# The ring of weights of a two-layer encoder: raw tiles of 1024 columns in three buffers instead of 2048 in two, and three split buffers instead of two

## The chip, the cores and the metric

The kernel runs on one core of a Trainium2 chip. The metric is the device time of one execution in microseconds (us), lower is better; the median of three runs is given. The engines are named as in the profile: PE is TensorE (matmuls), PEld its loads of the stationary operand, DVE VectorE, ACT ScalarE, POOL GpSimd, SP the queue that issues the DMAs.

## The reference

Two layers act on 512 tokens of width 1024, all in float32. Each layer is a gated feed-forward block, a mixer, and a second feed-forward block:

```python
for l in range(DEPTH):                                   # DEPTH = 2
    x = x + 0.5 * swiglu(rmsnorm(x, ffn1_norm[l]), ffn1_w_gate[l], ffn1_w_up[l], ffn1_w_down[l])
    h = rmsnorm(x, mix_norm[l])
    u = h @ w_in[l]
    ...
    y_conv = short_conv_mixer(c_x, c_b, c_c, conv_w[l])
    y_rwkv = rwkv7_mixer(rw_r, rw_k, rw_v, ...)          # a recurrence over the tokens, both directions
    y_ret = retention_mixer(rt_q, rt_k, rt_v, rt_g, positions, ret_gn_g[l])
    y_mla = mla_mixer(ml_qa, ml_kva, positions, ...)     # attention on latents
    x = x + jnp.concatenate([y_conv, y_rwkv, y_ret, y_mla], axis=-1) @ w_out[l]
    x = x + 0.5 * swiglu(rmsnorm(x, ffn2_norm[l]), ffn2_w_gate[l], ffn2_w_up[l], ffn2_w_down[l])
return rmsnorm(x, final_norm)

def swiglu(x, w_gate, w_up, w_down):
    return (jax.nn.silu(x @ w_gate) * (x @ w_up)) @ w_down   # width 2816 between
```

## The kernel before

Activations lie transposed in SBUF, eight tiles `x[d]` of 128 features by 512 tokens. A product of float32 numbers is made of three matmuls in the fast format fp32r (`mm3`, L338 to L340): weight and activation are each split in a high part and the rest, and hi·hi, hi·lo and lo·hi are added up in PSUM. The activation is split once (`xg`, the two halves `xh` and `xl`). The weights are split as they come, and this is the ring that the change is about:

- `load` (L331) takes a raw tile `w_raw` of 2048 columns by 128 partitions (1 MB) from a ring of two and fills it with one DMA on SP's queue.
- `split` (L320) takes a pair `w_hi`, `w_lo` of up to 1152 columns from a ring of two and fills it: ACT copies the raw columns to `w_hi` in fp32r (L327), DVE subtracts that from the raw columns into `w_lo` (L328). Both carry a high priority for the scheduler. A raw tile is mostly split in two calls of 1024 columns.
- A split pair of 1024 columns feeds 24 matmuls of 512 columns on PE. The pair comes free when the last of them has read it; the raw tile when its last split is done.

The callers: `ffn` takes a tile of 2048 columns for each of 22 blocks of the hidden width (gate `pg` in the first half, up `pu` in the second), then tiles of 1408 columns (704 KB) for the way down (`pd`), split as 768 and 640. In the mixer `proj` takes one tile of 2048 for two neighbouring projections (`pj`), keeps it in `self.cache`, and splits it in halves as they are needed, each with two instructions of 512 columns on ACT and DVE. `proj_nat` makes two products with the tokens on the partitions (`pn`): `wrv` (8 x 256 columns, one raw tile, two splits) and `wtv` (8 x 288 columns, two raw tiles of 1152, two splits); all four token blocks use both splits. `w_out` (`po`) loads 512 columns at a time. `retention` uses the two raw tiles as scratch (`ret_big`), one for each half `j` of its heads.

The order of instructions on each engine is not written by hand. A scheduler works it out when the program is built, from the program's order, the priorities and its own estimate of when buffers and operands are ready; each engine then runs its list in that order and waits at the head of it. In the mixer the scheduler puts several strands in one list: the projections, the recursion that inverts small triangular blocks (`rwkv_inverse`, L972 and L974 on DVE, 31 steps after one another, fed through DRAM by the DMAs `s<-NR`, `Lb<-s`, `Nb<-s`), the recurrence over eight chunks (`rwkv_chain`: on PE L1059, L1081, L1090, L1105, L1078, L1123 for each chunk, with copies on ACT, DVE and POOL between them), attention (`m_sc`, `m_ptp`, `m_po`) and retention. Both layers have the same list in the kernel before.

Of the kernel before, what the change touches and what calls it, by code (L numbers as in the profile page):

```python
# [27 lines left out]
MLA_TAGS = (("mm", "mm", "mm"), ("mm", "mm", "mm"), ("b", "a", "mm"), ("b", "a", "mm"))  # L28
H = 4
# [105 lines left out]
class K:  # L135
# [122 lines left out]
    def norm_part(self, d, gain, l, square=True):  # L258
# [15 lines left out]
        V.scalar_tensor_tensor(hl[:, 1], x, g, hl[:, 0].bitcast(F32), ALU.mult, ALU.subtract)  # L274
        self.xh.append(hl[:, 0])
# [66 lines left out]

    def ffn(self, l, which, then, between=None):
        nc, V, A = self.nc, self.nc.vector, self.nc.scalar
        wgu, wdn = self.I[f"gu{which}"], self.I[f"dn{which}"]
        for half in range(2):
            gh, gl = [], []
            for f in range(HALF):
                raw, self.first = self.first, None
                begin = raw is not None  # L350
                if raw is None:
                    raw = self.load(wgu[l, half * HALF + f], 2048)
                pg = self.ps("pg", "mm")
                pu = self.ps("pu", "b")
                for o, ps in ((0, pg), (1, pu)):
                    hi, lo = self.split(raw[:, 1024 * o:1024 * o + 1024], 1024, 512 if begin else 1024)
# [20 lines left out]
                gl.append(hl[:, 1])  # L377
            if between is not None:
# [34 lines left out]
class Mixers:  # L413
# [6 lines left out]
    def run(self):  # L420
# [4 lines left out]
        self.cache = None  # L425
# [60 lines left out]
    def proj_nat(self, src, n, dst):  # L486

        k, l = self.k, self.l
        half = KD // 2 * n
        if 2 * half <= 2048:  # L490
            raw = k.load(src, 2 * half)
            pieces = [k.split(raw[:, half * o:half * o + half], half, 2 * n) for o in range(2)]
        else:
            pieces = [k.split(k.load(src[:, half * o:half * o + half], half), half, 2 * n) for o in range(2)]
        mm = self.nc.tensor.matmul
        for tt in range(NT):
            ps = k.ps("pn", "mm")[:, 0:n]
# [95 lines left out]
    def retention(self):  # L593
# [682 lines left out]
```

## Time and profile before

| | |
|---|---|
| time, median of three runs | 2168.68 us (2167.41 to 2171.97) |
| the profiled execution's own time | 2169.86 us |
| its span, first to last instruction | 2168.1 us |
| mean granted clock of PE | 0.995 |
| busy: PE / PEld / DVE / ACT / POOL | 98% / 79% / 51% / 33% / 6% |
| moved by DMA | 204.68 MB, 94 GB/s on average |

The profile is of one execution. A busy PE counts each matmul from its start to its modelled end, and neighbouring matmuls overlap: a matmul of 512 columns is shown with 0.39 us, but the next one starts 0.23 us after it. What a wait costs is therefore read from start to start. Matmuls in plain float32 (scores, transposes, the recurrence) are shown as two records each.

### The profile page before, as it was taken

Reading aid. Unit: us, or ns where it says so; the run is one execution under the profiler, and the core shown is the slowest. Engines: PE = TensorE matmul, PEld = TensorE weight load, DVE = VectorE, ACT = ScalarE, POOL = GpSimd, SP = SyncE. Lnnn points to the kernel's source line nnn. Section 1 sums busy time; section 2 is a strip of 40 time slices with the busy share of each in tenths; the row PEclk is TensorE's granted clock in tenths of the full one; section 3 lists DMA queues with packets and bytes.
Section 4 is the critical chain, followed back from the end, with each engine's and each line's share of the span. In section 5 each row is a group of like instructions: output and inputs, shape, how many; then the busy total and the mean of one; then the engine's idle time right before and its main releaser. Section 6 shows DMA issues by size and latency. Waiting matters only on the chain.

```text
span 2168.1 us, 27576 instructions
## 1 busy us (share of the span) xinstructions
PE 2131.3 (98%) x11316; PEld 1714.9 (79%) x11316; DVE 1113.3 (51%) x1917; ACT 711.6 (33%) x1061; POOL 122.4 (6%) x146
## 2 busy tenths in 40 slices
PE   8999999999999999999999999999999999999997
PEld 7888888788666888888888888887886578888886
DVE  4454445676577543443544444457756865434433
ACT  4222223443233422222322222335323243222232
POOL 2000001000020100000100000010001210000001
PEclk9999999999999999999999999999999999999998
DMA  4223224144002322322322232242330122223222
GB/s 170 97 85 106 98 95 151 61 118 129 20 21 86 116 98 85 117 97 79 106 97 91 94 109 95 92 147 72 116 101 21 64 90 105 91 80 111 97 87 79
DMA packets 65294, 204.68 MB, mean 94 GB/s; under 512 B 26512, under 2 KB 26768, under 8 KB 50960
## 3 DMA queue, kind: packets, MB, share of 16 engines
q1 hardware_dynamic: 65168, 202.93, 28.5%
q8 instruction: 88, 1.44, 0.3%
q14 instruction: 38, 0.31, 0.0%
HBM read 191.37 MB, written 9.44 MB: 93 GB/s over the span
## 4 chain that ended last, share of the span: by engine, by line
PE 93%; DVE 4%; ACT 1%; DMA 1%; issue 1%; SPq 0%; DVEq 0%; ACTq 0%
PE pg L338 7%; PE pg L340 7%; PE pg L339 7%; PE pu L338 7%; PE pd L340 7%; PE pu L339 7%; PE pd L339 7%; PE pd L338 7%; PE pu L340 7%; PE pj L338 4%; PE pj L339 4%; PE pj L340 4%; PE po L338 1%; PE po L339 1%; PE po L340 1%; PE m_pq L758 1%
## 5 line engine op out<-in xcount | busy, mean ns | idle before, releaser
L327 ACT CAST w_hi<-w_raw 128x1024 fp32r<-128x1024 f32 (+4 forms) x446 | 367.4, 836 | 1132.1 <-PE pg L339 308.9
L328 DVE TENSOR_TENSOR w_lo<-w_raw,w_hi 128x1024 fp32r<-128x1024 f32 (+4 forms) x446 | 425.7, 962 | 229.4 <-ACT w_hi L327 220.1
L338 PE MATMUL pg<-xg,w_hi 128*128 128x512 f32 x704 | 275.5, 391 | 6.2 <-ACT w_hi L327 6.2
L340 PE MATMUL pg<-xg,w_lo 128*128 128x512 f32 x704 | 275.0, 391 | 0.0
L339 PE MATMUL pg<-xg,w_hi 128*128 128x512 f32 x704 | 274.9, 390 | 0.0
L338 PE MATMUL pu<-xg,w_hi 128*128 128x512 f32 x704 | 274.1, 389 | 0.4 <-ACT w_hi L327 0.4
L339 PE MATMUL pu<-xg,w_hi 128*128 128x512 f32 x704 | 274.2, 389 | 0.0
L340 PE MATMUL pu<-xg,w_lo 128*128 128x512 f32 x704 | 273.9, 389 | 0.0
L340 PE MATMUL pd<-g,w_lo 128*128 128x512 f32 x704 | 273.9, 389 | 0.0
L338 PE MATMUL pd<-g,w_hi 128*128 128x512 f32 x704 | 273.9, 389 | 0.0
L339 PE MATMUL pd<-g,w_hi 128*128 128x512 f32 x704 | 273.9, 389 | 0.0
L372 DVE TENSOR_TENSOR g<-pu,s 128x512 f32<-128x512 f32 x88 | 60.9, 692 | 274.0 <-PE pu L340 271.2
L369 DVE TENSOR_TENSOR s<-pg,rb 128x512 f32<-128x512 f32 x88 | 60.8, 691 | 206.5 <-PE pg L340 206.4
L338 PEld LDWEIGHTS pg<-xg,w_hi 128*128 128x128 f32 x704 | 132.7, 188 | 33.7 <-ACT w_hi L327 6.2
L340 PEld LDWEIGHTS pg<-xg,w_lo 128*128 128x128 f32 x704 | 132.7, 188 | 28.5 <-DVE w_lo L328 1.0
L339 PEld LDWEIGHTS pg<-xg,w_hi 128*128 128x128 f32 x704 | 132.7, 188 | 28.0 <-DVE xg L274 0.5
L338 PEld LDWEIGHTS pu<-xg,w_hi 128*128 128x128 f32 x704 | 132.2, 188 | 28.1 <-ACT w_hi L327 0.9
L340 PEld LDWEIGHTS pu<-xg,w_lo 128*128 128x128 f32 x704 | 132.2, 188 | 27.5 <-DVE w_lo L328 0.2
L339 PEld LDWEIGHTS pd<-g,w_hi 128*128 128x128 f32 x704 | 132.2, 188 | 27.5
L338 PEld LDWEIGHTS pd<-g,w_hi 128*128 128x128 f32 x704 | 132.2, 188 | 27.4
L340 PEld LDWEIGHTS pd<-g,w_lo 128*128 128x128 f32 x704 | 132.2, 188 | 27.4
L339 PEld LDWEIGHTS pu<-xg,w_hi 128*128 128x128 f32 x704 | 132.2, 188 | 27.3
(294 smaller groups left out, 2706.5 us busy)
## 6 DMA issues: line engine op xcount, KB each, us to landing
w_raw<-gu SPq DMA_DIRECT2D x87, 1024.0 KB, 4.8
w_raw<-dn SPq DMA_DIRECT2D x64, 704.0 KB, 4.2
w_raw<-win SPq DMA_DIRECT2D x22, 1024.0 KB, 5.1
w_raw<-wo SPq DMA_DIRECT2D x32, 256.0 KB, 2.8
xs<-x SPq DMA_DIRECT2D x16, 256.0 KB, 4.7
x<-xs SPq DMA_DIRECT2D x16, 256.0 KB, 5.7
w_raw<-wtv SPq DMA_DIRECT2D x4, 576.0 KB, 4.2
x<-xT SPq DMA_DIRECT2D x8, 256.0 KB, 5.9
```

Of the source, the lines that this page charges most:

```text
L327: self.split_hi = self.nc.scalar.copy(hi[:, s], raw[:, s])
L328: self.nc.vector.tensor_tensor(lo[:, s], raw[:, s], hi[:, s].bitcast(F32), ALU.subtract)
L338: T_.matmul(ps, hi, xh, start=start, stop=False)
L339: T_.matmul(ps, hi, xl, start=False, stop=False)
L340: T_.matmul(ps, lo, xh, start=False, stop=stop)
L369: V.tensor_tensor(s, pg, rb, ALU.mult)
L372: V.tensor_tensor(g, pu, s, ALU.mult)
L758: mm(pq, wq[i][:, P * h:P * h + P], qa[i], start=i == 0, stop=i == 2)
```

## The change

The raw ring has three tiles of 1024 columns in place of two of 2048; the split ring has three pairs of 1024 columns in place of two of 1152. Per partition these are 36 KB in place of 34 KB. Every load asks for at most 1024 columns (512 KB): a feed-forward block makes two loads, the way down loads 768 and 640 columns apart, `proj` loads its own 1024 columns and keeps no cache, `wrv` is loaded and split in two pieces as before but from two raw tiles, `wtv` in three pieces (3, 3 and 2 of the eight feature blocks: 864, 864 and 576 columns). `retention` takes two raw tiles for each of its halves where it took one, so four in all from a ring of three. The small tile `rq_v` has one buffer in place of two.

The functions `sums` and `seven` and the list `SEVEN` are new in the file, but `SEVEN` is empty for both halves, so `seven` is never called, and nothing calls `sums`: no instruction comes of them. `x_moved`, `xhl` and `gain` are notes in Python that only they would read.

```diff
+SEVEN = ((), ())
...
-        first = self.ring.tile([P, 2048], F32, name="w_raw", tag="w_raw", bufs=2)
-        self.first = first
+        self.first = first = [self.raw() for _ in range(2)]
...
-                nc.sync.dma_start(first[:, q:q + 512], I["gu1"][0, 0][:, q:q + 512])
-        nc.sync.dma_start(first[:, 1024:2048], I["gu1"][0, 0][:, 1024:2048])
+                nc.sync.dma_start(first[0][:, q:q + 512], I["gu1"][0, 0][:, q:q + 512])
+        nc.sync.dma_start(first[1], I["gu1"][0, 0][:, 1024:2048])
...
+    def raw(self, name="w_raw"):
+        return self.ring.tile([P, 1024], F32, name=name, tag="w_raw", bufs=3)
...
-        v = self.tmp.tile([P, 16], F32, name="rq_v", tag="rq_v" + who)[:, :n]
+        v = self.tmp.tile([P, 16], F32, name="rq_v", tag="rq_v" + who, bufs=1)[:, :n]
...
     def split(self, raw, n, piece=1024):
 
-        hi = self.ring.tile([P, 1152], F32R, name="w_hi", tag="w_hi", bufs=2)[:, :n]
-        lo = self.ring.tile([P, 1152], F32R, name="w_lo", tag="w_lo", bufs=2)[:, :n]
+        hi = self.ring.tile([P, 1024], F32R, name="w_hi", tag="w_hi", bufs=3)[:, :n]
+        lo = self.ring.tile([P, 1024], F32R, name="w_lo", tag="w_lo", bufs=3)[:, :n]
...
     def load(self, src, n):
-        raw = self.ring.tile([P, 2048], F32, name="w_raw", tag="w_raw", bufs=2)[:, :n]
+        raw = self.raw()[:, :n]
...
                 if raw is None:
-                    raw = self.load(wgu[l, half * HALF + f], 2048)
+                    raw = [self.load(wgu[l, half * HALF + f][:, 1024 * o:1024 * o + 1024], 1024) for o in range(2)]
...
             for d in range(KD):
-                raw = self.load(wdn[l, half, d], HALF * P)
                 pd = self.ps("pd", "a")
                 for a, b in ((0, 6), (6, HALF)):
-                    hi, lo = self.split(raw[:, P * a:P * b], P * (b - a))
+                    hi, lo = self.split(self.load(wdn[l, half, d][:, P * a:P * b], P * (b - a)), P * (b - a))
...
-        if self.cache is None or self.cache[0] != idx // 2:
-            n = min(2048, 1024 * len(WIN_COLS) - 2048 * (idx // 2))
-            self.cache = (idx // 2, k.load(k.I["win"][l, idx // 2][:, :n], n))
-        o = idx % 2
-        hi, lo = k.split(self.cache[1][:, 1024 * o:1024 * o + 1024], 1024, PIECE)
+        o = 1024 * (idx % 2)
+        hi, lo = k.split(k.load(k.I["win"][l, idx // 2][:, o:o + 1024], 1024), 1024, PIECE)
...
-        half = KD // 2 * n
-        if 2 * half <= 2048:
-            raw = k.load(src, 2 * half)
-            pieces = [k.split(raw[:, half * o:half * o + half], half, 2 * n) for o in range(2)]
-        else:
-            pieces = [k.split(k.load(src[:, half * o:half * o + half], half), half, 2 * n) for o in range(2)]
+        per = 1024 // n
+        pieces = []
+        for a in range(0, KD, per):
+            b = min(a + per, KD)
+            pieces.append(k.split(k.load(src[:, n * a:n * b], n * (b - a)), n * (b - a), 2 * n))
...
-            big = k.ring.tile([P, 2048], F32, name="ret_big", tag="w_raw", bufs=2)
+            big, big2 = k.raw("ret_big"), k.raw("ret_big2")
...
-            qd, kn = big[:, 1024:1536], big[:, 1536:2048]
+            qd, kn = big2[:, 0:512], big2[:, 512:1024]
```

The scheduler makes new lists from this. In the feed-forward blocks PE's list is the same as before but for a few matmuls at their ends; in the mixers it differs in many places, and the two layers no longer have the same list. PE has the same matmuls in both. Three places follow. Line numbers of the changed kernel are its own: its L344 to L346 are L338 to L340 of before, L333 and L334 are L327 and L328, L250 is L246, and those from L502 on are higher by 128.

**The projection after `wtv`, first layer.** On PE this is the end of the products `pn` with `wtv` and the start of the next projection. Before:

```order
L503 MATMUL pn<-w_lo,xg_2499 128x288
L504 MATMUL pn<-w_hi,xg_2499 128x288
L338 MATMUL pj<-xg_2130,w_hi 128x512
L339 MATMUL pj<-xg_2130,w_hi 128x512
L340 MATMUL pj<-xg_2130,w_lo 128x512
L338 MATMUL pj<-xg_2181,w_hi 128x512
```

Now:

```order
L631 MATMUL pn<-w_lo,xg_2574 128x288
L632 MATMUL pn<-w_hi,xg_2574 128x288
L344 MATMUL pj<-xg_2191,w_hi 128x512
L345 MATMUL pj<-xg_2191,w_hi 128x512
L344 MATMUL pj<-xg_2191,w_hi 128x512
L345 MATMUL pj<-xg_2191,w_hi 128x512
L346 MATMUL pj<-xg_2191,w_lo 128x512
```

The first two matmuls of the projection after it have moved ahead of the first one that reads `w_lo`. On DVE this `w_lo` stands within the inverting recursion (`tmpR`, `Rb`). Before:

```order
L566 TENSOR_TENSOR rcb<-rc,rb 128x512
L567 TENSOR_TENSOR rsb<-rs,rb 128x512
L972 TENSOR_TENSOR tmpR<-Nb,Rb 128x192
L328 TENSOR_TENSOR w_lo<-w_raw,w_hi 128x512
L974 TENSOR_TENSOR Rb<-Rb,tmpR 128x24x8
```

Now:

```order
L694 TENSOR_TENSOR rcb<-rc,rb 128x512
L695 TENSOR_TENSOR rsb<-rs,rb 128x512
L1100 TENSOR_TENSOR tmpR<-Nb,Rb 128x192
L334 TENSOR_TENSOR w_lo<-w_raw,w_hi 128x512 x2
L1102 TENSOR_TENSOR Rb<-Rb,tmpR 128x24x8
```

It has not moved: it stands behind the eighth step's first half of the recursion in both.

**The first step of the recurrence, first layer.** On PE, from the state update of the first chunk (L1105, now L1233) to the first use of that state in the next chunk (L1078, now L1206). Before:

```order
L1105 MATMUL zy_3396<-ch_3394 64x64 x2
L1078 MATMUL zy_3464<-Sd,KQ_2514 128x128
L1078 MATMUL zy_3464<-Sd,KQ_2515 128x128
L1123 MATMUL zy_3395<-ch_3393,Gm 64x64
...
L1123 MATMUL zy_3396<-ch_3394,Gm 64x64
L1078 MATMUL zy_3465<-Sd,KQ_2516 128x128
```

Now:

```order
L1233 MATMUL zy_3479<-ch_3477 64x64 x2
L250 MATMUL m_pb<-con_t,m_fckv 128x128 x4
L851 MATMUL m_pk<-m_kr,con_t 128x512
L830 MATMUL m_ss<-con_t,m_sq 128x1 x4
L1206 MATMUL zy_3547<-Sd,KQ_2589 128x128
L1251 MATMUL zy_3478<-ch_3476,Gm 64x64
...
L870 MATMUL m_pv<-m_wkv,m_lat 128x256 x4
L876 MATMUL m_pkn<-m_lat,m_wkv 128x512
L1206 MATMUL zy_3548<-Sd,KQ_2591 128x128
```

Matmuls of the attention's latents now stand ahead of both L1206.

**The last step of the recurrence, first layer.** On PE, around the solve (L1090, now L1218) and the outputs (L1123, now L1251) of the eighth chunk. Before:

```order
L781 MATMUL m_sc<-m_kT,m_qT 128x512
L646 MATMUL ret_po<-ret_ms,ret_v 64x256
L665 MATMUL ret_ss<-con_t,ret_sq 128x2 x4
L646 MATMUL ret_po<-ret_ms,ret_v 64x256 x3
L1090 MATMUL zy_3912<-ch_3910,NR_3049 64x64
...
L781 MATMUL m_sc<-m_kT,m_qT 128x512
L1123 MATMUL zy_3912<-ch_3910,Gm 64x64
```

Now:

```order
L909 MATMUL m_sc<-m_kT,m_qT 128x512
L1218 MATMUL zy_3995<-ch_3993,NR_3132 64x64
...
L1218 MATMUL zy_3996<-ch_3994,NR_3133 64x64
L1251 MATMUL zy_3995<-ch_3993,Gm 64x64
...
L909 MATMUL m_sc<-m_kT,m_qT 128x512 x3
```

The score matmul between solve and outputs has moved behind the outputs, and the retention's matmuls ahead of the solve are gone from there. The second layer's list is alike at all three places, but with the four `ret_ss` still ahead of the solve. One more difference is only counted here: in both layers the block `psN` of 124 small matmuls, whose results feed the recursion, stands seven matmuls of a projection later than before.

## Rows read from the trace of the kernel before

**Rows 1.** Busy time by stretch: length, then PE, PEld, DVE, ACT, POOL; clock; DMA

```profile
0.00:370.00 370.00, 363.39 (x1597) 300.02 (x1598) 169.42 (x228) 120.16 (x160) 18.84 (x17) 1.00 0.34 113
370.00:675.00 305.00, 296.16 (x2251) 222.66 (x2251) 210.06 (x501) 114.61 (x210) 28.58 (x47) 0.99 0.25 75
675.00:1440.00 765.00, 765.00 (x3392) 631.36 (x3391) 337.62 (x436) 233.36 (x308) 26.75 (x20) 1.00 0.30 99
1440.00:1745.00 305.00, 297.04 (x2264) 223.51 (x2264) 211.64 (x504) 115.21 (x212) 28.32 (x47) 0.99 0.25 78
1745.00:2168.00 423.00, 409.69 (x1820) 337.32 (x1816) 184.57 (x252) 128.27 (x173) 19.88 (x15) 0.98 0.28 95
```

**Rows 2.** Waits of PE: total us, times, longest us

```profile
PE pg L338 <- ACT w_hi L327: 6.2, 1, 6.2
PE m_sc L781 <- ACT m_p L786: 5.8, 4, 1.7
...
PE pj L340 <- DVE w_lo L328: 2.7, 2, 1.7
...
PE pn L502 <- ACT w_hi L327: 1.0, 2, 0.5
PE zy L1078 <- ACT Yn L1132: 0.9, 2, 0.5
PE zy L1078 <- DVE Sd L1115: 0.8, 2, 0.4
PE pj L338 <- ACT w_hi L327: 0.5, 2, 0.2
PE pn L503 <- DVE w_lo L328: 0.4, 2, 0.2
PE pu L338 <- ACT w_hi L327: 0.4, 1, 0.4
```

**Rows 3.** Timeline of PE at the block psN: start, duration, what, count

```profile
453.19 2.14 PE L940 MATMUL psN<-KQ,KB 64*64 64x64 f32 x124
```

**Rows 4.** Timeline of PE at the first product with wrv

```profile
411.82 0.39 PE L340 MATMUL pj<-xg,w_lo 128*128 128x512 f32 x1
412.69 0.51 PE L502 MATMUL pn<-w_hi,xg 128*128 128x256 f32 x2 [0.48 <-ACT w_hi L327]
```

**Rows 5.** Timeline of ACT, the splits behind wrv

```profile
426.22 1.14 ACT L327 CAST w_hi<-w_raw 128x512 fp32r<-128x512 f32 x2 [8.31 <-PE pn L504]
```

**Rows 6.** Timeline of PE at the projection after wtv

```profile
473.55 0.40 PE L338 MATMUL pj<-xg,w_hi 128*128 128x512 f32 x1
473.78 0.40 PE L339 MATMUL pj<-xg,w_hi 128*128 128x512 f32 x1
475.90 0.50 PE L340 MATMUL pj<-xg,w_lo 128*128 128x512 f32 x1 [1.72 <-DVE w_lo L328]
```

**Rows 7.** Timeline of DVE, blocks for the recursion, its start, and that w_lo

```profile
454.67 2.48 DVE L945 TENSOR_TENSOR NR<-psN,con_t 128x512 f32<-128x512 f32 x4
...
468.31 0.21 DVE L972 TENSOR_TENSOR tmpR<-Nb,Rb 128x31 f32<-128x31 f32 x1 [5.81 <-DMA Nb<-s]
...
475.15 0.69 DVE L328 TENSOR_TENSOR w_lo<-w_raw,w_hi 128x512 fp32r<-128x512 f32 x1
```

**Rows 8.** Timeline of PE in the last step of the recurrence

```profile
653.21 0.68 PE L1090 MATMUL zy<-ch,NR 64*64 64x64 f32 x16
653.82 1.12 PE L781 MATMUL m_sc<-m_kT,m_qT 128*128 128x512 f32 x2
```

**Rows 9.** Timeline of DVE, the copy between solve and outputs there

```profile
654.14 0.40 DVE L1093 TENSOR_SCALAR ch<-zy 64x256 f32<-64x256 f32 x1
```

**Rows 10.** DMA issues: queue, count, size, median us from issue to landing

```profile
w_raw<-win SPq DMA_DIRECT2D x2, 512.0 KB, 4.5
ret_big<-big SPq DMA_DIRECT2D x4, 256.0 KB, 3.8
```

**Rows 11.** Timeline of POOL, the product that waits for the second of these

```profile
531.61 1.29 POOL L605 TENSOR_TENSOR ret_big<-ro_t,ret_big 128x512 f32<-128x512 f32 x1 [4.08 <-DMA ret_big<-big]
```

More of the change, by code (lines that the diff above doesn't have):

```diff
@@ L340, in mm3, with sums @@
         T_.matmul(ps, lo, xh, start=False, stop=stop)
+    def sums(self):
+        V, A = self.nc.vector, self.nc.scalar
+        self.T = []
+        gain, l = self.gain
+        for i in range(KD // 2):
+            b = []
+            for d in (i, i + KD // 2):
+                t = self.ft("t_b")
+                A.activation(t, self.x[d], AF.Copy, scale=self.v(gain, l, d))
+                b.append((t[:, 0:256], t[:, 256:512]))
+            (b11, b12), (b21, b22) = b
+            s = [self.ft("t_s") for _ in range(2)]
+            T1, T2, T3, T4 = (t[:, 256 * q:256 * q + 256] for t in s for q in range(2))
+            V.tensor_tensor(T1, b12, b11, ALU.subtract)
+            V.scalar_tensor_tensor(T2, b22, -1.0, T1, ALU.mult, ALU.subtract)
+            V.scalar_tensor_tensor(T3, b22, -1.0, b12, ALU.mult, ALU.subtract)
+            V.tensor_tensor(T4, T2, b21, ALU.add)
+            out = []
+            for t in s:
+                if len(self.T) < 2 or not self.x_moved:
+                    hl = self.vt("T", shape=(P, 2, 2, 256), dt=F32R)
+                    hl = [hl[:, q] for q in range(2)]
+                else:
+                    hl = [self.ft("T", shape=(P, 2, 256), dt=F32R) for q in range(2)]
+                for q in range(2):
+                    a = t[:, 256 * q:256 * q + 256]
+                    A.copy(hl[q][:, 0], a)
+                    V.tensor_tensor(hl[q][:, 1], a, hl[q][:, 0].bitcast(F32), ALU.subtract)
+                out += hl
+            self.T.append(out)
@@ new lines, in seven, with parts, product, taken @@
+    def seven(self, src, rb):
+        nc, V, A = self.nc, self.nc.vector, self.nc.scalar
+        Q = 512
+        first, second = self.raw(), self.raw()
+        r11, r21, r22, r12 = (t[:, q:q + Q] for t in (first, second) for q in (0, Q))
+        for o, t in ((0, r11), (2, r21), (3, r22), (1, r12)):
+            nc.sync.dma_start(t, src[:, Q * o:Q * o + Q])
+        def parts(*srcs):
+            hi = self.ring.tile([P, 1024], F32R, name="w_hi", tag="w_hi", bufs=3)
+            lo = self.ring.tile([P, 1024], F32R, name="w_lo", tag="w_lo", bufs=3)
+            a = 0
+            for t in srcs:
+                z = slice(a, a + t.shape[1])
+                A.copy(hi[:, z], t)
+                V.tensor_tensor(lo[:, z], t, hi[:, z].bitcast(F32), ALU.subtract)
+                a = z.stop
+            return [(hi[:, q:q + Q], lo[:, q:q + Q]) for q in range(0, a, Q)]
+        with self.tc.high_priority(offset=AHEAD):
+            w11, = parts(r11)
+            V.tensor_tensor(r11, r11, r21, ALU.subtract)
+            V.tensor_tensor(r21, r21, r22, ALU.subtract)
+            r2, r4 = self.ft("w_s2"), self.ft("w_s4")
+            V.scalar_tensor_tensor(r2, r11, -1.0, r22, ALU.mult, ALU.subtract)
+            V.tensor_tensor(r4, r12, r2, ALU.add)
+            S1, S2 = parts(r21, r2)
+            S4, S3 = parts(r4, r11)
+            w22, w12 = parts(second)
+        y, x, z = self.ps("f_y", "mm"), self.ps("f_x", "b"), self.ps("f_z", "b")
+        tok = lambda h, j: [t[:, :, 256 * j:256 * j + 256] for t in self.xhl[4 * h:4 * h + 4]]
+        T = lambda n: [t[n - 1] for t in self.T]
+        def product(ps, w, b, start):
+            hi, lo = w
+            for i in range(4):
+                c = slice(P * i, P * i + P)
+                nc.tensor.matmul(ps.rearrange("p (q t) -> p q t", q=2), hi[:, c], b[i], start=start and i == 0,
+                                 stop=False, skip_group_check=True)
+                nc.tensor.matmul(ps[:, 0:256], lo[:, c], b[i][:, 0], start=False, stop=i == 3, skip_group_check=True)
+        def taken(ps):
+            t = self.ft("f_m")
+            A.copy(t, ps)
+            return t
+        product(y, w11, tok(0, 0), True)
+        m1 = taken(y)
+        product(z, S1, T(1), True)
+        m5 = taken(z)
+        product(y, S2, T(2), False)
+        u2 = taken(y)
+        product(z, S4, tok(1, 1), False)
+        product(y, S3, T(3), False)
+        u3 = taken(y)
+        product(x, w12, tok(1, 0), True)
+        product(y, w22, T(4), False)
+        s, g = self.ft("s"), self.ft("g")
+        def fold(o, t):
+            V.tensor_tensor(o, t[:, 0:256], t[:, 256:512], ALU.add)
+        V.tensor_tensor(u2, z, u2, ALU.add)
+        fold(s[:, 256:512], u2)
+        V.tensor_tensor(u3, u3, m5, ALU.add)
+        fold(g[:, 256:512], u3)
+        V.tensor_tensor(m1, x, m1, ALU.add)
+        fold(s[:, 0:256], m1)
+        V.tensor_tensor(s, s, rb, ALU.mult)
+        A.activation(s, s, AF.Silu)
+        A.copy(g[:, 0:256], y[:, 256:512])
+        V.tensor_tensor(g[:, 0:256], y[:, 0:256], g[:, 0:256], ALU.add)
+        V.tensor_tensor(g, g, s, ALU.mult)
+        return g
@@ L348, in ffn @@
             for f in range(HALF):
+                if f in SEVEN[half]:
+                    g = self.seven(wgu[l, half * HALF + f], rb)
+                    hl = self.vt(f"g{f}", dt=F32R)
+                    A.copy(hl[:, 0], g)
+                    V.tensor_tensor(hl[:, 1], g, hl[:, 0].bitcast(F32), ALU.subtract)
+                    gh.append(hl[:, 0])
+                    gl.append(hl[:, 1])
+                    continue
                 raw, self.first = self.first, None
@@ L355, in ffn @@
                 for o, ps in ((0, pg), (1, pu)):
-                    hi, lo = self.split(raw[:, 1024 * o:1024 * o + 1024], 1024, 512 if begin else 1024)
+                    hi, lo = self.split(raw[o], 1024, 512 if begin else 1024)
                     if begin and o == 1:
@@ L377, in ffn @@
                 gl.append(hl[:, 1])
+                if f == 0 and half == 0:
+                    pass
             if between is not None:
@@ L460, in x_back @@
         k = self.k
+        k.x_moved = True
         for d in range(0, KD, 2):
```

10 lines of the change are left out of this document (6 added, 4 removed).

## The prediction

> **What bounds the kernel now.** I read the busy time by stretch first, because one average hides stages with different limits [rows 1]. PE is busy for the whole of the 765 us around the second and third feed-forward block, and idle for 6.6 us in the first stretch, 8.8 and 8.0 us in the two mixers, and 13.3 us in the last one. So the feed-forward blocks run at PE's own pace, and whatever the ring can give lies in the start and the mixers. The last stretch ends in a normalization that the ring has no part in. The view of waits then says who ends PE's idle time [rows 2]. The longest, 6.2 us, is the first load and split of the program, which the change does as before. The waits for weights that remain are `pj` for `w_lo` (2.7 us in 2), `pn` for `w_hi` and `w_lo` (1.0 and 0.4), `pj` and `pu` for `w_hi` (0.5 and 0.4). Others in that list are strands of the mixer: scores for the softmax on ACT (5.8), the recurrence for its state and its copies (0.9 and 0.8).
>
> Matmuls overlap in the records, so I price a wait from start to start. Two neighbours of 512 columns start 0.23 us apart (473.55, 473.78) [rows 6]. At the first product with `wrv` the starts are 411.82 and 412.69: 0.87 less 0.23 is 0.64 us lost, where the idle time shows 0.48 [rows 4]. A wait costs its idle time and 0.16 us.
>
> **The waits of a ring of two.** Seven waits, the ones of `pn`, `pj` L338 and `pu`, come to 2.3 us idle [rows 2], with 7 x 0.16 us 3.4 us. What ends them is a split that ran late because both pairs were taken: the cast behind `wrv` stood 8.3 us until `pn` let a pair go [rows 5]. With a third pair the splits run one tile further ahead in the lists of ACT and DVE, so I take all seven as gone: 0.6 us at the start (0.44 + 0.16), and (1.0 + 0.4 + 0.5)/2 + 3 x 0.16 = 1.4 us in each mixer.
>
> **What the next wait takes back.** The largest weight wait is not one of the ring. `pj` stands for `w_lo` from 473.78 to 475.90, 1.9 us lost [rows 6]. That subtraction ran at 475.15 on DVE, behind the first steps of the recursion, which began at 468.31 when `Nb` landed; that transfer follows from the blocks NR that DVE read from `psN` from 454.67 on [rows 7]. In the new list the `w_lo` stands at the same step of the recursion. So its time hangs on `psN`, not on buffers. `psN` began at 453.19 [rows 3]; it comes 1.4 us earlier by the waits removed and 7 x 0.23 = 1.6 us later by the seven matmuls put ahead of it. The recursion starts when it did, and PE arrives earlier and waits longer. Only the two matmuls now placed ahead of this wait are kept, 2 x 0.23 = 0.5 us per mixer. So of 2.8 us in both mixers 0.9 us stays. If the recursion moved with PE, 2 x (1.4 + 0.5) = 3.7 us would; if the wait went altogether, 3.0 us more (2.7 + 2 x 0.16).
>
> **The recurrence.** In its first step PE waits for the state and for a copy on ACT, 0.9 + 0.8 us idle in four waits [rows 2], 2.3 us with 4 x 0.16. In the new list `m_pb`, `m_pk` and `m_ss` stand ahead of the first, `m_pv` and `m_pkn` ahead of the second. `m_pk` alone is a float32 matmul of 512 columns like `m_sc`, shown with 1.12 us [rows 8], more than the longest of these waits (0.5 us). I take all 2.3 us as gained; no less than 0.
>
> In the last step something is lost. Between solve and outputs PE did a score matmul from 653.82 on [rows 8], while DVE made the copy that the outputs need: it began at 654.14 and took 0.40 us, so it was done at 654.54 [rows 9]. Now nothing stands there, and PE waits from 653.82 to about 654.6, 0.8 us in each layer, 1.6 us in all. Bounds: 0, if the copy comes sooner, and twice that, since ahead of the solve the cover is thinner too and its copy costs the same kind of wait.
>
> The scores behind it are placed anew. Their waits (5.8 us in 4 [rows 2], 6.4 with the starts) may vanish or double; the rows have no reason for either, and I take 0.
>
> **What costs nothing.** A load of 512 KB lands 4.5 us after its issue [rows 10]; three tiles of 24 matmuls are 16.6 us of PE, so it is covered three times. If that cover were gone, each load longer than its tile's 5.5 us would show on PE. The casts of `wtv` are five in place of four, on an engine that is idle for two thirds of the time. `rq_v` in one buffer orders instructions that DVE runs one after another anyway. Retention's fourth raw tile must wait until the first half is done with its own: 3.8 us for the load [rows 10] and 1.29 us on POOL [rows 11], 5.1 us. From the last `ret_po` that reads the first half's to the first that reads the second's, PE has 64 matmuls in the first layer and 49 in the second. Six and four groups of eight small ones at 0.61 us (653.21 to 653.82 [rows 8]) and eight or more of 256 columns at about a quarter to a half of `m_sc`'s 1.12 us make an estimate of 5 us or more in either. Covered, barely in the second; without cover 5.1 us each.
>
> The Trainium skill has a rule against smaller loads: "DMA: Bandwidth & Descriptors", section "Rules for kernel authors", wants at least 1 MiB in each DMA for the full rate. The rows don't bear it out as a bound here: 512 KB in 4.5 us are 117 GB/s from one load alone [rows 10], and no stretch moves more than 113 [rows 1]. By the row the sum is unchanged; by the rule it would be the last rival below.
>
> **The sum.** -0.6 - 0.9 - 2.3 + 1.6 = -2.2 us. Against the profiled execution's 2169.86 us that is 2167.7; the median of the runs is 1.2 us lower, so 2166.5 us. Its own range, by the bounds on the recursion, the last step and half of the score waits, is 2162 to 2170.
>
> **The rivals.**
> *All waits for weights were the ring's.* Then 3.4 + 3.0 us go, and 2.3 us in the recurrence without the loss at its end: 8.7 us, 2160.0 us. For it: six of the nine rows name `w_hi` or `w_lo`. Against it: the largest hangs on the recursion [rows 6, 7]. "Perfetto Trace Analysis" of the Trainium skill, section "Optimization Strategy", says that the same gap repeating on the engine that should be full can mean too few buffers; by that rule this rival would hold. Here the gaps don't repeat at the pace of the tiles: 765 us of feed-forward have none [rows 1].
>
> *The waits only move.* The recursion's wait takes everything, and new waits in the recurrence give back its 2.3 us: only the start's 0.6 us stays, 2168.1 us. For it: each list is waited through in order, and what PE gains ahead of a chain it spends at the chain.
>
> *The recurrence runs out of cover (the other side).* Attention now starts a step earlier and is used up earlier, so later steps stand bare. The price of a bare step is 2.3/2 = 1.15 us for the state and the copy and 0.8 us between solve and outputs, 2.0 us. With three such steps in each layer it is 6 x 2.0 - 0.6 - 0.9 - 2.3 = +8.2, 2176.9 us. It decides from the fifth bare step in both layers together (4.3 + 3.8 = 8.1 us). Against it: the new list has something between most of the hand-overs; only the last step is plainly bare.
>
> *The loads come late.* If one load at a time were in flight, a tile of 640 columns, 15 x 0.23 = 3.5 us on PE, would wait 1.0 us for a load of 4.5, 64 times: over 2230 us. Against it: three tiles, and DMA busy for 25 to 34% [rows 1].
>
> **How the numbers follow.** Forecast 0.47, all the ring's 0.20, moved 0.20, bare recurrence 0.11, late loads 0.02. A measurement of this kernel can tell about 0.2%, 4.3 us, from no change: faster means under 2164.3, slower over 2173.0. Faster: nearly all of the first rival and a fifth of the forecast, 0.29. Slower: most of the last two and a small part of the forecast, 0.13. Same: 0.58. The range from 2159.5 to 2171.5 takes in the first rival and leaves out the last two.
>
> **What the profile will show.** Right: no waits of `pn` for weights, none of `pu` at 20 us, the `pj` wait for `w_lo` at least as long as before (2 to 3.5 us per layer), the recursion's start within 1 us of 468 less the start's gain, no waits of the first chunk's L1206, and new waits of about 0.8 us ahead of the last L1251. Wrong: if the recursion starts clearly earlier, the take-back is too large; if score waits (L909) differ by more than 3 us, they decide the sign; waits of feed-forward matmuls for `w_hi` behind a DMA would bring the last rival.

## The result and the profile after

The changed kernel is **slower**: 2184.07 us (median of 5 runs, 2176.55 to 2187.39) against 2170.85 us (5 runs), a ratio of 1.0059 with a 95% interval of 1.0042 to 1.0076. The forecast was 2166.5 us, the range ended at 2171.5 us, and the chance given to slower was 0.13.

The profiled execution has a span of 2185.6 us and a mean granted clock of 0.988 (before: 2168.1 us and 0.995). By stretch, cut so that each holds the same work as in [rows 1] (length, then busy time of PE, PEld, DVE, ACT, POOL; granted clock; DMA):

```profile
0.00:370.00 370.00, 363.53 (x1597) 300.15 (x1598) 172.91 (x230) 121.70 (x162) 19.73 (x17) 1.00 0.37 113
370.00:686.00 316.00, 301.14 (x2247) 226.69 (x2246) 212.97 (x504) 114.34 (x210) 27.79 (x47) 0.97 0.26 75
686.00:1450.00 764.00, 764.00 (x3393) 630.60 (x3393) 338.49 (x432) 234.06 (x308) 27.02 (x20) 1.00 0.32 99
1450.00:1762.00 312.00, 302.92 (x2259) 229.52 (x2257) 213.31 (x507) 114.98 (x213) 28.87 (x48) 0.97 0.27 77
1762.00:2185.00 423.00, 410.15 (x1827) 337.75 (x1825) 182.06 (x247) 128.32 (x172) 20.10 (x15) 0.98 0.30 93
```

All of the loss lies in the two mixers: 316 and 312 us where it was 305 twice. PE is idle there for 14.9 and 9.1 us (8.8 and 8.0 before), and its clock is 0.97 where it was 0.99. The feed-forward stretch of 764 us has no idle time and a clock of 1.00, so the smaller loads cost nothing there. The largest group of them (KB each, us from issue to landing):

```profile
w_raw<-gu SPq DMA_DIRECT2D x175, 512.0 KB, 3.7
```

Who ends the waits of PE (us in total, times, longest):

```profile
PE m_sc L909 <- ACT m_p L914: 8.0, 9, 2.1
...
PE zy L1233 <- DVE ch L1221: 5.1, 4, 2.6
...
PE pj L346 <- DVE w_lo L334: 2.6, 2, 1.3
PE zy L1251 <- DVE ch L1221: 2.2, 2, 1.2
PE zy L1218 <- DVE ch L1213: 2.1, 2, 1.4
PE kk_ss L1007 <- ACT kk_sq L1004: 2.0, 2, 1.0
...
PE pg L344 <- ACT xg L278: 0.5, 1, 0.5
```

Against [rows 2] the waits of `pn` and `pu` for weights are gone, as the change means them to be (`pn` still waits 0.6 us in two for DVE, where the profile names `tmpR` and not a weight). New are `kk_ss`, `L1251` and `L1218`, and the scores and `L1233` wait longer. Where the clock fell is seen in stretches of 10 us:

```profile
405.00:415.00 10.00, 9.02 (x46) 7.16 (x44) 4.95 (x6) 8.42 (x14) 0.00 (x0) 1.00 0.00 0
415.00:425.00 10.00, 10.00 (x61) 10.00 (x61) 5.03 (x18) 3.02 (x4) 0.00 (x0) 0.66 0.38 118
635.00:645.00 10.00, 7.39 (x91) 5.29 (x85) 9.13 (x19) 2.81 (x6) 4.40 (x6) 0.83 0.14 47
660.00:670.00 10.00, 7.05 (x49) 3.89 (x48) 9.45 (x34) 1.41 (x4) 1.01 (x1) 0.83 0.52 175
1497.00:1507.00 10.00, 10.00 (x61) 10.00 (x61) 5.03 (x18) 3.01 (x4) 0.00 (x0) 0.66 0.34 120
1620.00:1630.00 10.00, 10.00 (x160) 8.56 (x159) 2.06 (x3) 1.96 (x4) 0.39 (x1) 0.70 0.01 2
1742.00:1752.00 10.00, 6.21 (x14) 2.41 (x12) 10.00 (x28) 5.13 (x11) 1.43 (x1) 0.74 0.00 0
```

The falls at 1620 us and at 542 us (0.83 from 537 to 547 us) stand behind the 64 `psR` and eight `bo_ps`, where the kernel before has one in each layer too; the others are at places where its trace has 1.00.

From 415 us on PE is busy all the time, at a clock of 0.66: it does the same products at a lower pace. What it did just before, on PE's timeline:

```profile
413.15 0.28 PE L632 MATMUL pn<-w_hi,xg 128*128 128x256 f32 x1
414.42 2.49 PE L1007 MATMUL kk_ss<-con_t,kk_sq 128*128 128x2 f32 x16 [0.98 <-ACT kk_sq L1004]
416.77 0.56 PE L630 MATMUL pn<-w_hi,xg 128*128 128x256 f32 x1
417.13 0.41 PE L631 MATMUL pn<-w_lo,xg 128*128 128x256 f32 x1
417.34 0.41 PE L632 MATMUL pn<-w_hi,xg 128*128 128x256 f32 x1
```

One us of waiting, then eight matmuls of two columns (16 records) in some 2.3 us. Behind them the products of 256 columns start 0.21 us apart, where they started 0.12 us apart ahead of it (413.03 to 413.15). In the kernel before, PE lost 0.64 us and more at the first `pn` [rows 4], came to `kk_ss` later and did not wait there:

```profile
414.24 0.28 PE L503 MATMUL pn<-w_lo,xg 128*128 128x256 f32 x1
414.36 1.86 PE L879 MATMUL kk_ss<-con_t,kk_sq 128*128 128x2 f32 x16
416.08 0.36 PE L504 MATMUL pn<-w_hi,xg 128*128 128x256 f32 x1
```

So the wait that the third pair removed came back one step later, beside small matmuls, and in this execution the clock fell behind it. The kernel before shows such a fall without any wait, at its 64 `psR` and eight `bo_ps`:

```profile
533.68 2.12 PE L1006 MATMUL psR<-NR,RT_Y 32*32 32x32 f32 x128
535.73 2.41 PE L1029 MATMUL bo_ps<-con_t,rk_r 128*128 128x2 f32 x16
538.00 0.77 PE L339 MATMUL pj<-xg,w_hi 128*128 128x512 f32 x1
538.58 0.63 PE L340 MATMUL pj<-xg,w_lo 128*128 128x512 f32 x1
539.00 0.63 PE L338 MATMUL pj<-xg,w_hi 128*128 128x512 f32 x1
539.43 0.63 PE L339 MATMUL pj<-xg,w_hi 128*128 128x512 f32 x1
```

The products of 512 columns start 0.43 us apart there and 0.23 us elsewhere [rows 6]: the lower of the two levels of the clock, 1.2 GHz in place of 2.4. This was in the trace before the prediction, and the prediction didn't read it.

### The profile page after: what moved, and what is told of

The parts are those of the page before. It is cut to its first block, busy times and chain, and to the rows that moved or that the text cites. A ratio compares the mean times of both kernels' runs of the same rounds, so it can differ in the third digit from the quotient of the medians.

```text
span 2185.6 us, 28113 instructions
## 1 busy us (share of the span) xinstructions
PE 2141.7 (98%) x11316; PEld 1724.7 (79%) x11316; DVE 1119.7 (51%) x1919; ACT 713.4 (33%) x1063; POOL 123.5 (6%) x146
## 4 chain that ended last, share of the span: by engine, by line
PE 93%; DVE 4%; ACT 1%; DMA 1%; issue 1%; SPq 0%; DVEq 0%; ACTq 0%
PE pg L344 7%; PE pg L345 7%; PE pg L346 7%; PE pu L344 7%; PE pu L346 7%; PE pd L344 7%; PE pd L346 7%; PE pu L345 7%; PE pd L345 7%; PE pj L344 4%; PE pj L346 4%; PE pj L345 4%; PE po L344 1%; PE po L345 1%; PE po L346 1%; PE m_sc L909 1%
## 5 line engine op out<-in xcount | busy, mean ns | idle before, releaser
L333 ACT CAST w_hi<-w_raw 128x1024 fp32r<-128x1024 f32 (+5 forms) x448 | 368.1, 834 | 1106.7 <-PE pg L345 315.7
L334 DVE TENSOR_TENSOR w_lo<-w_raw,w_hi 128x1024 fp32r<-128x1024 f32 (+5 forms) x448 | 428.7, 964 | 204.6 <-ACT w_hi L333 195.1
L344 PE MATMUL pg<-xg,w_hi 128*128 128x512 f32 x704 | 275.7, 392 | 6.5 <-ACT w_hi L333 6.0
L346 PE MATMUL pg<-xg,w_lo 128*128 128x512 f32 x704 | 274.9, 390 | 0.0
L344 PE MATMUL pu<-xg,w_hi 128*128 128x512 f32 x704 | 274.1, 389 | 0.0
L346 PE MATMUL pu<-xg,w_lo 128*128 128x512 f32 x704 | 273.9, 389 | 0.0
L346 PE MATMUL pd<-g,w_lo 128*128 128x512 f32 x704 | 273.9, 389 | 0.0
L344 PE MATMUL pd<-g,w_hi 128*128 128x512 f32 x704 | 273.9, 389 | 0.0
L344 PEld LDWEIGHTS pg<-xg,w_hi 128*128 128x128 f32 x704 | 132.8, 189 | 34.4 <-ACT w_hi L333 6.0
L346 PEld LDWEIGHTS pg<-xg,w_lo 128*128 128x128 f32 x704 | 132.7, 188 | 28.0 <-DVE w_lo L334 0.3
L346 PEld LDWEIGHTS pd<-g,w_lo 128*128 128x128 f32 x704 | 132.1, 188 | 27.5
L346 PEld LDWEIGHTS pu<-xg,w_lo 128*128 128x128 f32 x704 | 132.1, 188 | 27.5
L344 PEld LDWEIGHTS pd<-g,w_hi 128*128 128x128 f32 x704 | 132.1, 188 | 27.4
L344 PEld LDWEIGHTS pu<-xg,w_hi 128*128 128x128 f32 x704 | 132.1, 188 | 27.4
```

The lines of the kernel that those rows point to most:

```text
L333: self.split_hi = self.nc.scalar.copy(hi[:, s], raw[:, s])
L334: self.nc.vector.tensor_tensor(lo[:, s], raw[:, s], hi[:, s].bitcast(F32), ALU.subtract)
L344: T_.matmul(ps, hi, xh, start=start, stop=False)
L346: T_.matmul(ps, lo, xh, start=False, stop=stop)
```

## The experiments

Each run lists its mean granted clock. (1 - clock) x span is the time that the clock can have cost; for the profiled execution (1 - 0.988) x 2185.6 = 26.2 us. Some 8 us of it (0.02 x 423) lie in the last stretch of either kernel, where PE waits anyway, so it is an upper bound. Its differences between kernels are a guide and not exact: the last stretch's share alone differs by up to 2 us between the kept profiles, and the clock is listed to 0.001, 2.2 us. A single run's split is rough (the runs of e5 differ by 2.6 us in time and by 6.8 us in this "rest"); a mean over runs is good to 1 or 2 us. "Rest" is the mean time less the clock's share.

| kernel | median us (runs) | ratio to before, 95% interval | clock, us | rest, us |
|---|---|---|---|---|
| before, beside e1 to e4 | 2170.31 (16) | | 12.3 | 2158.5 |
| before, beside e5 to e8 | 2170.32 (20) | | 12.9 | 2157.3 |
| before, beside e9 to e13 | 2170.61 (15) | | 13.0 | 2157.8 |
| before, beside e14 and e15 | 2170.39 (20) | | 13.4 | 2157.2 |
| the changed kernel | 2184.07 (5) | 1.0059 (1.0042 to 1.0076) | 22.7 | 2160.4 |
| e1 new rings, PE's list of before | 2177.77 (6) | 1.0033 (1.0021 to 1.0045) | 20.3 | 2157.1 |
| e2 old rings, PE's new list | 2195.77 (4) | 1.0114 (1.0098 to 1.0130) | 30.7 | 2165.0 |
| e3 changed, work ahead of kk_ss | 2183.40 (5) | 1.0056 (1.0043 to 1.0069) | 22.3 | 2161.0 |
| e4 changed, kk_ss later | 2177.63 (11) | 1.0030 (1.0022 to 1.0039) | 17.8 | 2159.5 |
| e5 new rings, PE, DVE, ACT as before | 2164.30 (8) | 0.9974 (0.9964 to 0.9984) | 10.3 | 2154.2 |
| e6 before, bo_ps spread | 2167.28 (11) | 0.9989 (0.9980 to 0.9997) | 9.5 | 2158.4 |
| e7 e5 with bo_ps spread | 2162.68 (5) | 0.9966 (0.9954 to 0.9978) | 9.1 | 2153.6 |
| e8 changed, one copy on DVE earlier | 2186.58 (6) | 1.0077 (1.0065 to 1.0089) | 24.0 | 2162.7 |
| e9 before, 144 small together | 2217.00 (4) | 1.0211 (1.0197 to 1.0225) | 27.1 | 2189.5 |
| e10 before, 144 small spread | 2207.27 (4) | 1.0167 (1.0152 to 1.0183) | 15.4 | 2191.8 |
| e12 raw part alone, old lists | 2172.34 (11) | 1.0007 (0.9998 to 1.0015) | 14.4 | 2157.7 |
| e13 raw part alone, free lists | 2188.71 (5) | 1.0081 (1.0069 to 1.0094) | 22.7 | 2165.8 |
| e14 new rings, PE and ACT as before | 2165.51 (10) | 0.9975 (0.9965 to 0.9984) | 11.5 | 2154.0 |
| e15 new rings, PE and DVE as before | 2173.94 (11) | 1.0018 (1.0008 to 1.0027) | 15.2 | 2159.2 |

Of the 12.3 us between the means of the changed kernel and of before (first line), 10.4 are clock and 1.9 rest by this split. The profiled executions show both parts in the mixers, which are 18 us longer: PE is idle for 7.1 us more, and by the stretches the clock can have cost some 13 us more (0.03 x 628 against 0.01 x 610). The two add up to more than the 18 us, so neither is exact; the clock is the larger.

**Rings and lists apart (e1, e2).** A list is fixed by a table: for each engine the order in which the instructions stood in another build, by their place in the program, and each is tied behind its forerunner, in issue order only.

```diff
+    for e, text in LISTS.items():
...
+        order = np.cumsum(np.frombuffer(zlib.decompress(base64.b85decode(text)), np.int16))
...
+        for a, b in zip(order, order[1:]):
+            tc.add_manual_dep(mine[b], mine[a].name, mybir.DependencyInfo(mybir.DependencyClass.NoSync, mybir.DependencyReason.DATA), reason="pin")
```

> The changed kernel with PE's list fixed to that of the kernel before, matmul for matmul; rings, loads and tiles are the changed ones, and the other engines' lists are free. Theory O (the order of the list lost the time, by waits that stand beside small matmuls and by TensorE's clock, which falls behind them): the time goes back to that of before, 2166 to 2171 us, mean granted clock 0.994 or more. Theory B (the smaller loads or the shared ring lost it): as the changed kernel, 2180 to 2187 us.

> The kernel before with PE's list fixed to that of the changed one; rings, loads and tiles are those of before. Theory O: slow as the changed kernel or worse, 2178 to 2190 us, mean granted clock 0.991 or less, since a ring of two also waits where the new list reads ahead. Theory B: as before, 2167 to 2172 us.

Neither theory stands alone. PE's new list is bad with either ring (2195.77 against 2170.31 us on the old rings, 2184.07 against 2177.77 us on the new), but e1 is still 7.5 us over before. Its rest is 1.4 us lower; its clock cost 8 us more. Its waits name the place:

```profile
PE m_sc L909 <- ACT m_p L914: 5.7, 2, 2.8
PE pn L630 <- ACT w_hi L333: 3.4, 1, 3.4
...
PE kk_ss L1007 <- ACT kk_sq L1004: 2.0, 2, 1.0
```

The lists of ACT and DVE had been left free, and new ones came with the new rings: in the first layer the third cast of `wtv` (466.03 us) stood behind a copy (`Nb`, 464.96 us) that had waited 11.6 us for the DMA `Lb<-s`, and the score matmuls waited 2.8 us at one place in each layer (5.7 us in all, as much as the 5.8 us in four waits of before).

**The lists of the other engines (e5, e14, e15).**

> The changed kernel with the lists of PE, DVE and ACT all fixed to those of the kernel before (only the five splits of wtv in each layer are placed freely, since before has four; the lists of POOL and of the DMA queue are free). Theory O (the lists lost the time, not the rings): the long waits of the first experiment go (3.4 us for a split behind wtv, 2.8 us twice in the scores) and with them the falls of the clock behind them: 2165 to 2171 us, mean granted clock 0.994 or more. Theory B (ring and smaller loads): it stays near the first experiment, 2175 to 2180 us, with the clock at 0.991 or 0.992.

It came out at 2164.30 us, a little below what was expected and 6.0 us under before; of the 5.7 us between the means 3.1 are rest and 2.6 clock. The new rings under the old lists make the kernel faster (the lists of POOL and of the DMA queue were left free); theory B is out.

> The changed kernel with the lists of PE and ACT fixed to those of before, DVE's free. Theory A (ACT's list, the cast of wtv behind the copy that waits for a DMA, carries the loss): 2164 to 2168 us. Theory D (DVE's list carries it, by the score waits of 2.8 us in each layer and the clock behind them): 2172 to 2178 us. If both carry a part: about 2169 to 2172 us.

> The changed kernel with the lists of PE and DVE fixed to those of before, ACT's free. Theory A: 2172 to 2178 us, with a wait of 3 us or more of pn for w_hi. Theory D: 2164 to 2168 us, with score waits of 5.8 us as before. If both carry a part: about 2169 to 2172 us.

Against e1 (2177.77 us), which has PE's old list, ACT's list alone gives 12.3 us, DVE's alone 3.8: theory A. But the wait that it named for e15, `pn` for `w_hi`, is not there; one place that shows the loss is `kk_ss`, which waits 2.0 us in two in e15 and not at all in e5 and e14. ACT's timeline shows why. First the kernel with three old lists, then the one with ACT's list free:

```profile
389.00 1.14 ACT L333 CAST w_hi<-w_raw 128x512 fp32r<-128x512 f32 x2 [0.82 <-ACT w_hi L333]
390.16 1.28 ACT L981 ACT_TABLE_LOAD   x1
395.67 1.85 ACT L981 ACTIVATE sg<-ps_wa,vec 128x512 f32<-128x512 f32 x3 [4.23 <-PE ps_wa L977]
```

```profile
394.37 1.14 ACT L333 CAST w_hi<-w_raw 128x512 fp32r<-128x512 f32 x2 [4.30 <-issue]
395.53 1.28 ACT L981 ACT_TABLE_LOAD   x1
396.82 1.27 ACT L981 ACTIVATE sg<-ps_wa,vec 128x512 f32<-128x512 f32 x2
```

PE's timeline at `kk_ss`, in the same two kernels:

```profile
413.19 1.87 PE L1007 MATMUL kk_ss<-con_t,kk_sq 128*128 128x2 f32 x16
```

```profile
414.26 2.36 PE L1007 MATMUL kk_ss<-con_t,kk_sq 128*128 128x2 f32 x16 [0.99 <-ACT kk_sq L1004]
```

In the old list the casts come early, because a pair is free, and ACT loads the table for its sigmoid in the time in which it waits for `ps_wa`: the sigmoid starts at 395.67 us. The free list uses the third pair to place one more cast ahead of the sigmoid. The cast starts at 394.37 us, after ACT has stood for 4.3 us, the table load is behind it, and the sigmoid starts 1.15 us later than in the old list, though `ps_wa` came at the same time. Against the kernel before this is not late. There the ring of two held the cast up until the same moment:

```profile
394.39 1.14 ACT L327 CAST w_hi<-w_raw 128x512 fp32r<-128x512 f32 x2 [4.31 <-PE pj L339]
...
396.84 1.27 ACT L853 ACTIVATE sg<-ps_wa,vec 128x512 f32<-128x512 f32 x2
```

So `kk_sq`, at the end of that chain, starts at 413.51 us in the kernel before and in e15, at 413.66 us in the changed kernel and at 412.36 us in e5. The free list takes from ACT what the third pair could have given it; PE, which no longer waits for weights, comes earlier and waits for `kk_sq`. That ACT's list loses at this place is shown by the profiles of e14 and e15, which have the same list on PE: they part mostly at `kk_ss`, by about 3 us in the first layer.

**The wait beside kk_ss (e3, e4).** In e3 eight useless matmuls stand ahead of `kk_ss`; in e4 `kk_ss` stands behind the nine `pn` that follow it.

```diff
+        for _ in range(8):
+            mm(sp[:, 256:512], k.xh[0][:, 0:P], k.xh[0][:, 0:256], start=True, stop=True)
```

> The changed kernel with eight useless matmuls of 256 columns added on PE ahead of the first kk_ss in each layer (16 in all, about 1.9 us of work, written to columns of that tile that nobody reads); all lists are otherwise fixed to those of the changed kernel. Theory K (the wait for kk_sq beside the small kk_ss costs mostly by the clock that falls behind it, 0.66 in the next 10 us): the stretches from 415 and from 1497 us have a clock of 1.00 and the kernel is 4 to 7 us faster than the changed one, though it does more work, 2177 to 2180 us. Theory W (only the wait itself costs): the work fills the wait of 1.0 us and adds nothing or up to 2 us, 2184 to 2186 us.

> The changed kernel with the eight kk_ss of each layer moved behind the nine pn that follow them; all lists are otherwise those of the changed kernel. Theory K: no wait, and clock 1.00 from 415 and from 1497 us: 6 to 9 us faster than the changed kernel, 2175 to 2178 us. Theory W: the two waits of 1.0 us go and nothing else, 2182 us.

e4 came out as theory K has it: 6.4 us by the medians for waits of 2.0 us; of the 5.9 us between the means 4.9 are clock. e3 did not. In its profile the clock from 415 us is 1.00 and from 1497 us 0.83, but it fell at other places too (0.83 from 470 us), and the runs' mean is that of the changed kernel, against 4 to 7 us less by theory K. Filling the wait is not enough on average, and why moving `kk_ss` is stays open.

**A copy of the recurrence (e8).** The edit is of DVE's list; the two splits taken out here come later, behind the update of the state.

```diff
+L1221 TENSOR_SCALAR ch_3845<-zy_3847 64x256
 L779 TENSOR_TENSOR ret_o<-ret_po,ret_g 128x512
-L641 TENSOR_TENSOR ys_5055<-c_y,ys_5055 128x512
-L334 TENSOR_TENSOR w_lo<-w_raw,w_hi 128x512
-L1221 TENSOR_SCALAR ch_3845<-zy_3847 64x256
```

> The changed kernel with one edit of DVE's list, at the sixth chunk of the recurrence in the first layer: the copy ch (L1221), for which PE waits 2.6 us at 639 us, is taken ahead of the retention's output, a split of ys and one of w_lo; all other lists are those of the changed kernel. Theory W: about 1.5 to 2.5 us less, 2181.5 to 2182.5 us, with the clock as it was. Theory K: also the clock of 0.66 in the 5 us behind that wait comes back, 3 to 4.5 us less, 2179.5 to 2181 us. No change would mean that the wait moves to the next step of the recurrence.

No gain: 2186.58 us. The wait of 2.6 us went, and one for the retention's masked scores `ret_ms` took its place, on the same engine (DVE stood 3.1 us for a cast of ACT ahead of them):

```profile
PE ret_po L774 <- DVE ret_ms L767: 3.1, 1, 3.1
PE zy L1233 <- DVE ch L1221: 2.9, 4, 1.0
```

**Small matmuls where nothing waits (e6, e9, e10).** In e6 the eight `bo_ps` are set one by one between the next projection matmuls. e9 and e10 add 16 small matmuls to each of nine tiles of a feed-forward block, in a row or apart.

```diff
+                        if small:
+                            c = KD * o + k
+                            nc.tensor.matmul(sm[:, 2 * c:2 * c + 2], self.con("ident"), self.con("hm2"), start=True, stop=True)
```

> The kernel before with one edit of PE's list in each layer: the eight small bo_ps, which stand in one block right behind the 64 small psR, are set one by one between the projection matmuls that follow; all other lists as they were. No wait of the profile goes away by this. Theory K (the clock falls behind a stretch of small matmuls): the clock of 0.66 from 537 us and of 0.83 from 1608 us rises to 1.00, and the kernel is 2 to 5 us faster than before, 2165 to 2168 us. Theory W (only waits cost): no change, 2170 us, or slightly slower.

> The kernel before with 144 useless matmuls of two columns added in the third feed-forward block, where PE has no wait at all: at nine places, 16 in a row, each time behind the last matmul of a pu (they read two constant tiles and write a PSUM tile that nobody reads); all other lists are those of before. By the block of eight bo_ps (2.41 us) a row of 16 takes about 4.6 us, 41 us in all. Theory K (a stretch of small matmuls lowers the clock behind it, though PE never waits): 1.7 to 3.4 us more at each place, 15 to 31 us, so 2226 to 2243 us, granted clock 0.981 to 0.988, and slower than the next run by those 15 to 31 us. Theory W: 2211 us and as the next run.

> The same 144 useless matmuls at the same nine tiles of the third feed-forward block, but one behind every third large matmul instead of 16 in a row. Theory K: the clock stays where it was in before (0.994 to 0.995); 2195 to 2211 us by the price of a small matmul among large ones, which no row shows, and 15 to 31 us of granted clock less lost than in the run before this one. Theory W: no difference between the two but that price.

e6 gains 3.0 us, all of it clock (12.9 to 9.5 us; the rest is no lower), though no wait is touched; from 537 and from 1608 us its profile has 1.00. The gain is small: two of the eleven runs, the profiled one among them, took some 6 us more than the others' median, at 0.994 and 0.993. e9 and e10 do the same work, and e9 is 9.7 us slower, with 11.7 us more lost to the clock. That is less than the 15 to 31 us expected: in e9's profile the clock fell with only some of the nine rows (in e10's it is 1.00 from 745 to 890 us, all through the changed tiles). The first row of e9 (16 matmuls, two records each), with PE never idle:

```profile
757.25 0.40 PE L340 MATMUL pu<-xg,w_lo 128*128 128x512 f32 x1
757.48 4.05 PE L368 MATMUL small<-con_t 128*128 128x2 f32 x32
761.39 0.77 PE L338 MATMUL pg<-xg,w_hi 128*128 128x512 f32 x1
761.96 0.63 PE L339 MATMUL pg<-xg,w_hi 128*128 128x512 f32 x1
762.39 0.63 PE L340 MATMUL pg<-xg,w_lo 128*128 128x512 f32 x1
```

By stretch the clock is 0.77 with this row and 1.00 with another of 16 (at 792.89 us, 3.63 us long):

```profile
755.00:770.00 15.00, 15.00 (x70) 12.80 (x69) 2.56 (x4) 1.82 (x3) 0.00 (x0) 0.77 0.20 70
785.00:800.00 15.00, 15.00 (x84) 13.00 (x83) 4.44 (x5) 3.17 (x4) 0.00 (x0) 1.00 0.21 71
```

`kk_ss` goes both ways as well. In e1 PE waits 1.0 us for `kk_sq` as in the changed kernel, and the clock stays up. In e6, which has before's list there, PE does not wait at `kk_ss` (it waited 0.7 us for weights just ahead, as in the kernel before), and the clock falls. First the stretch of e1, then `kk_ss` and the stretch of e6:

```profile
415.00:425.00 10.00, 10.00 (x86) 10.00 (x86) 7.04 (x23) 2.22 (x3) 0.00 (x0) 1.00 0.32 110
```

```profile
415.63 2.55 PE L879 MATMUL kk_ss<-con_t,kk_sq 128*128 128x2 f32 x16
```

```profile
415.00:425.00 10.00, 10.00 (x61) 10.00 (x60) 5.40 (x19) 4.16 (x6) 0.00 (x0) 0.66 0.35 118
```

So the wait at `kk_ss` is neither needed for the fall nor enough for it, and one execution can't tell what a place costs; only the mean clocks of the table can. What decides whether the clock falls at a place stays open.

**Which part of the change (e12, e13).** The raw part alone: raw ring of three, loads of 512 KB, split ring of two.

```diff
-        return self.ring.tile([P, 1024], F32, name=name, tag="w_raw", bufs=3)
+        return self.ring.tile([P, 1152], F32, name=name, tag="w_raw", bufs=3)
-        hi = self.ring.tile([P, 1024], F32R, name="w_hi", tag="w_hi", bufs=3)[:, :n]
+        hi = self.ring.tile([P, 1152], F32R, name="w_hi", tag="w_hi", bufs=2)[:, :n]
...
-        per = 1024 // n
+        per = KD // 2
```

> The raw part alone: raw ring of three (tiles of 1152 columns, so that wtv keeps its two loads), loads of 512 KB, retention with two raw tiles for each half; the split ring stays at two of 1152. The lists of PE, DVE and ACT are those of before. If the third split pair is what made the kernel with three old lists 6 us faster, the waits of pn and pu for weights stay and this is as before, 2168 to 2172 us; if the raw tiles and the smaller loads did it, 2163 to 2166 us; if smaller loads cost something that the third pair hid, over 2172 us.

> The same raw part alone with all lists left to the scheduler, which then moves 528 of PE's 9890 matmuls against before (the changed kernel: 617). Theory O (what the scheduler makes of new rings is what costs): slower than the run before this one, and than the kernel before, 2174 to 2190 us, with the clock at 0.992 or less. If only the third split pair brings the bad list: as before, 2168 to 2172 us.

With the old lists the raw part does nothing (the interval holds 1), so what is left for the 6 us of e5 is the third pair, with `wtv` in three pieces. With free lists the raw part costs 16 us more: here too the scheduler answered a new ring with new lists, and these were no better than the changed kernel's. The third pair alone, beside two raw tiles of 2048 columns, was not tried; it would take 40 KB per partition where the changed rings take 36.

**Both findings together (e7).**

> The changed rings with the three lists of before and the spread bo_ps of the experiment before this one: what both findings together give. Theories O and K: 2161 to 2167 us, faster than both kernels, with the highest mean clock of all (0.996). Theory B: over 2172 us. Theory W with O: as the kernel with the three old lists alone.

2162.68 us is the fastest of all, 0.34% under before: the new rings, three old lists, and `bo_ps` spread. The mean clock (0.995 to 0.997 in five runs) leaves little but the last stretch.

## Why the prediction was wrong

- **What failed is the step "A wait costs its idle time and 0.16 us", and with it the clock, which the sum puts at nothing.** It prices a wait as if TensorE ran at one speed. Beside small matmuls the clock can fall, behind a wait (the rows at 415 us, 0.66) and without any (e6, e9 and e10). The Trainium skill, "TensorE: Matmul & The Clock Gate", section "HAM oscillation — how this bites in real kernels", tells of a kernel whose clock falls in its waits for DMAs. The changed kernel's clock also fell behind a wait (0.83 from 635 us, where PE waits 2.6 us), but that of e9 with no idle time at all (757 us). Of the 12.3 us lost, some 10.4 are clock by the split of the table.
- **The idle time failed too.** The sum's terms for the mixers come to -0.9 - 2.3 + 1.6 = -1.6 us; measured are 7.1 us more of idle time. The points below say where.
- **"The waits of a ring of two": right that they go.** All waits of `pn` and `pu` for weights, and of `pj` L338 for `w_hi`, are gone. By themselves the rings are worth more than the forecast gave: e5's rest is 3.1 us lower and its clock cost 2.6 us less, where the sum had 0.6 + 0.9 for them. At the start nothing was kept: a wait of 0.5 us for `xg` came instead.
- **"What the next wait takes back": half right.** The wait of `pj` for `w_lo` stayed, 2.6 us in two. But the recursion did not start when it did: at 471.39 us in place of 468.31 [rows 7], since `psN` stands later and behind the lowered clock (it starts at 457.31 us in place of 453.19). With the old lists (e5) it began at 467.60 us, 0.7 us earlier: it hangs on `psN`, and moves with it. (The bound 2 x (1.4 + 0.5) is 3.8 us, not 3.7; the sum doesn't use it.)
- **The recurrence: right in its first step, too small after it.** No wait of the first chunk's L1206 is left. At the last chunk L1251 waits 2.2 us in two, more than the 0.8 us each, and the solve (L1218) 2.1 us. Not foreseen was the sixth chunk: 2.6 us for a copy that DVE's new list put behind splits and the retention's output.
- **Scores: taken as 0, measured +2.2 us** of idle time and five more waits.
- **What costs nothing: right for the loads, wrong for ACT's casts.** No wait of PE names a load and the feed-forward stretches stayed whole. Retention's tile is waited for on POOL (21.4 us in three, 16.2 in four before), and PE shows no wait for its DMA. But the casts were put at nothing because ACT is idle for two thirds of the time, an average that says nothing of their place in its list: with PE's old list, ACT's old list alone is worth 12.3 us (e14 against e1).
- **The rivals.** "The recurrence runs out of cover" had the right side (2176.9 us) and part of the place, but only by idle time: it too lacks the clock. The order of ACT's casts, which carried most of what was still lost once PE had its old list, was none of the four. What PE's new list costs (6.3 us, e1 against the changed kernel) is not traced to single places. The prediction compared PE's lists, and DVE's at one place; ACT's it didn't.

## What to carry to other kernels

A deeper ring changes two things where a scheduler makes the lists: the buffers and every engine's order; here the first was worth -6 us and the second +20 us, and only fixing the old lists on the new rings told them apart. Casts that run further ahead stand in front of something else on their engine, so compare the list of the engine that fills the ring, not only that of the engine that empties it. And read the granted clock beside each wait: a stretch of small matmuls can cost again behind its end, and setting them apart among large ones (e6) was worth 3 us with no wait removed.

## What the hardware showed that was not expected

The clock can fall behind small matmuls though PE is never idle (4.05 us of matmuls of two columns, then 0.43 us from one product of 512 columns to the next in place of 0.23), and not each time: equal rows in one execution gave 0.77 and 1.00 over 15 us. With it the time of one kernel spreads: five runs of the changed kernel lie between 2176.55 and 2187.39 us with clocks from 0.992 to 0.988, while their rest differs by no more than 2.5 us.
